# The first norm of a hybrid decoder layer: unit-stride normalisation, norm weights spread over the partitions by the tensor engine, and another written order up to the keys and values

## The chip, the core and the metric

The kernel runs on one core of a Trainium2 chip. The core has a tensor engine (PE) for matrix products, a vector engine (DVE), a scalar engine (ACT), GpSimd (POOL) and a sync engine (SP) that here issues nearly all the DMAs. The metric is the device time of one execution in microseconds (us), and less is better.

## The reference, cut to what matters

One decoder layer over 512 tokens of width 1024: a norm, a projection by `w_in`, two attention branches, an output projection with a residual, then a mixture of experts and a last norm. The change touches the first norm and the first columns of the projection.

```python
def rms_norm(x, g):
    xf = x.astype(jnp.float32)
    y = xf * lax.rsqrt(jnp.mean(xf * xf, axis=-1, keepdims=True) + EPS)
    return (y * g.astype(jnp.float32)).astype(x.dtype)
...
    proj = h @ w_in
    q_f, k_f, v_f, f_logit, q_s, k_s, v_s, gl_f, gl_s = jnp.split(proj, SPLIT_POINTS, axis=-1)
...
        h = rms_norm(x, attn_norm[l])
        x = x + hybrid_mixer(h, positions, w_in[l], b_forget[l], b_gate[l], attn_sinks[l],
                             w_proj_fox[l], w_proj_swa[l], w_out[l])
        h = rms_norm(x, ffn_norm[l])
        x = x + hier_moe(h, w_group[l], b_group[l], w_expert[l], b_expert[l], w1[l], w3[l], w2[l])
    return rms_norm(x, final_norm)
```

## The kernel before

The 512 tokens are four tiles of 128 (t = 0 to 3); the width of 1024 is eight chunks of 128, in two halves of four chunks (k = 0, 1). A product in full precision is made of three matrix products of rounded parts: every operand is split into a high part (a copy with rounding, on ACT) and a low part (the operand less its high part, a subtraction). `mm3` (lines 298 to 301) issues the three: high by high, high by low weights, low activations by high weights.

From line 386 on the order is written by hand: each of PE, DVE, ACT, POOL and SP takes its instructions in the order in which the Python code issues them (`tc.manual_schedule`). An instruction that waits holds up all that stand behind it on its engine.

**Loads.** SP issues x tile 0, the norm weights `gn` (one row read for each of 128 partitions, 512 KB), the two weight units `kv_0` and `kv_1` (each 4 chunks of 256 columns and 8 more, line 172), x tile 1, small inputs, x tiles 2 and 3, then the first unit of the sliding-window queries (`qs0_0`). Three raw buffers and three pairs of split buffers (pools `raw` and `ws`) go round: `next_unit` (line 193) splits the next unit (`hi` on ACT at line 185, `lo` on DVE, or on GpSimd for `kv_1`, line 186) and issues another load.

**The first norm.** `mean_square(t)` squares a tile on ACT with the sum as a by-product (line 242), then finds the reciprocal root: one small DVE instruction, a power on GpSimd (line 230), four more small DVE instructions (lines 231 to 234). `norm(t)` multiplies x, the root and the weights in two DVE instructions of 512 columns (line 251), reading x and writing `hn` with strides, since chunk c here holds the columns c, c+8, c+16 and so on. `transpose_h(t)` turns the tile by four PE transposes per half (line 257), and each half is split into `hT_hi` on ACT (line 260) and `hT_lo` on DVE (line 261).

**Keys and values.** For each tile, 24 products (8 chunks by 3) against `kv_0` and `kv_1` build one accumulator of 264 columns. After the fourth chunk of tile t (`START_T`) stand the transposes of tile t+1 and then the norm of tile t+2, so that a norm is written more than a tile ahead of its transposes. A tile's result is read out by one ACT copy and two DVE instructions (lines 417 to 419). The unit `qs0_0` is split after tile 1, the positions are cast to floats there (line 422), and six steps of the rotary angles (`angles`, with two small PE transposes at lines 271 and 272) stand between tiles 2 and 3. 30 transposes of the identity (line 396) run at the very start. After tile 3 come two more units, the rest of the angles, the masks, and the products of the queries (`acc_qs`).

Of the kernel before, what the change touches and what calls it, by code (L numbers as in the profile page):

```python
# [11 lines left out]
F32 = mybir.dt.float32  # L12
# [3 lines left out]
AF = mybir.ActivationFunctionType  # L16
OP = mybir.AluOpType
# [14 lines left out]
UNIT = 264  # L32
# [8 lines left out]
LAG = (2, 3)  # L41
WAIT = 2
REST = (2, 3)
START_T = 3
WARM = 30
ANGLES_AT = 6
FORGET_AT = 13
ROUNDS = 5
# [22 lines left out]
def bcast_rows(ap, n):  # L71

    return bass.AP(tensor=ap.tensor, offset=ap.offset, ap=[[0, P], [1, n]])
# [24 lines left out]
def kernel(ctx: ExitStack, tc: tile.TileContext, a: dict, out: bass.AP, dbg=None):  # L98
    nc = tc.nc
    pools = Pools(tc)  # L100
    ctx.callback(pools.close_all)
    v, act, pe, gp = nc.vector, nc.scalar, nc.tensor, nc.gpsimd
    dbg = dbg or {}

    x2 = a["x"][0]
    out2 = out[0]
    w_in = a["w_in"][0]
# [17 lines left out]
    def o_tile(name):  # L125
        return ps.tile([P, 512], F32, tag="o", name=name, bufs=2)
# [4 lines left out]
    ssq, rinv, rtmp = cst[:, 16:20], cst[:, 20:24], cst[:, 24:32]  # L131
    mcst = main.tile([P, 64], F32, name="mcst")
    sinks, bgate, pos, bfor, neg_sinks = (mcst[:, x:y] for x, y in ((0, 8), (8, 24), (24, 28), (32, 40), (40, 48)))
# [1 line left out]
    stage_i = xin.tile([P, P], I32, name="stage_i")  # L135
    bg_rows, inv_rows = stage[:16, 0:128], stage[:, 128:160]
    x_sb = [xin.tile([P, D], F32, tag=f"x{t}", name=f"x_sb{t}") for t in range(NT)]
    gn = xin.tile([P, D], F32, name="gn")
    w_in_pc = w_in.rearrange("(p c) n -> p c n", c=NC)


    units = {}
    for name in ORDER:
        kind, i = name.rstrip("0123456789"), int(name[-1]) if name[-1].isdigit() else 0
# [47 lines left out]

    def next_unit(wait=0):

        if len(halves_of) < len(unit_names):
            key = unit_names[len(halves_of)]
            halves_of[key] = split(raws[key], key, wait)
            load_unit()

    nc.sync.dma_start(x_sb[0], x2[0:P, :])  # L200
    nc.sync.dma_start(gn, bcast_rows(a["attn_norm"][0], D))
    load_unit()
    nc.sync.dma_start(x_sb[1], x2[P:2 * P, :])
    load_unit()
    nc.sync.dma_start(stage_i[:NT, :], a["positions"][0].rearrange("(t p) -> t p", p=P))
    nc.sync.dma_start(inv_rows, bcast_rows(a["inv_freq"], 32))
    nc.sync.dma_start(bg_rows, a["b_gate"][0].rearrange("g (b p) -> (g b) p", p=P))
    nc.sync.dma_start(bfor, bcast_rows(a["b_forget"], 8))
    nc.sync.dma_start(sinks, bcast_rows(a["attn_sinks"], NH))
    for t in range(2, NT):  # L210
        nc.sync.dma_start(x_sb[t], x2[t * P:(t + 1) * P, :])
    load_unit()
    nc.sync.dma_start(g_ffn, a["ffn_norm"][0].rearrange("(p c) -> p c", c=NC))

    ident = const.tile([P, P], F32, name="ident")
    make_identity(nc, ident)
    mhalf = const.tile([P, NT], F32, name="mhalf")
# [7 lines left out]
    def rsqrt_mean(dst, ssq, tmp):  # L225

        n = ssq.shape[-1]
        ms, e = tmp[:, 0:n], tmp[:, n:2 * n]
        v.tensor_scalar(ms, ssq, 1.0 / D, EPS, op0=OP.mult, op1=OP.add)
        gp.tensor_tensor(dst, ms, mhalf[:, 0:n], op=OP.pow)  # L230
        v.tensor_tensor(e, dst, dst, op=OP.mult)
        v.tensor_tensor(e, e, ms, op=OP.mult)
        v.tensor_scalar(e, e, -0.5, 1.5, op0=OP.mult, op1=OP.add)
        v.tensor_tensor(dst, dst, e, op=OP.mult)

    hn = [xin.tile([P, NC, P], F32, tag=f"hn{t}", name=f"hn{t}") for t in range(NT)]
    hT_hi = main.tile([P, NC, T], F32R, name="hT_hi")
    hT_lo = main.tile([P, NC, T], F32R, name="hT_lo")
    xt = xin.tile([P, 2 * NT], F32, name="xt")

    def mean_square(t):
        act.activation(hn[t].rearrange("q c p -> q (c p)"), x_sb[t], AF.Square, accum_out=ssq[:, t:t + 1])
        rsqrt_mean(rinv[:, t:t + 1], ssq[:, t:t + 1], xt[:, 2 * t:2 * t + 2])

    def norm(t):

        r = rinv[:, t:t + 1]
        x_pc, g_pc = (z.rearrange("q (p c) -> q p c", c=NC) for z in (x_sb[t], gn))
        h_pc = hn[t].rearrange("q c p -> q p c")
        for c in (slice(0, 4), slice(4, 8)):  # L250
            v.scalar_tensor_tensor(h_pc[:, :, c], x_pc[:, :, c], r, g_pc[:, :, c], op0=OP.mult, op1=OP.mult)

    def transpose_h(t):
        for k in range(2):
            pst = pt_tile(f"hT_ps{t}_{k}")
            for c in range(4):
                pe.transpose(pst[:, c * P:(c + 1) * P], hn[t][:, 4 * k + c], ident)
            d = (slice(None), slice(4 * k, 4 * k + 4), slice(t * P, (t + 1) * P))
            p3 = pst.rearrange("p (c n) -> p c n", c=4)
            act.activation(hT_hi[d], p3, AF.Copy)  # L260
            v.tensor_tensor(hT_lo[d], p3, hT_hi[d].bitcast(F32), op=OP.subtract)
# [36 lines left out]
    def mm3(o, l_hi, l_lo, r_hi, r_lo, first, last):  # L298
        pe.matmul(o, l_hi, r_hi, start=first, stop=False, skip_group_check=True)  # L299
        pe.matmul(o, l_hi, r_lo, start=False, stop=False, skip_group_check=True)  # L300
        pe.matmul(o, l_lo, r_hi, start=False, stop=last, skip_group_check=True)  # L301
# [86 lines left out]
    vs = main.tile([P, NT, P], F32, name="vs")  # L388
# [3 lines left out]


    warm = o_tile("warm")
    for _ in range(WARM):
        pe.transpose(warm[:, 0:P], ident, ident)
    mean_square(0)
    norm(0)
    next_unit()
    transpose_h(0)  # L400
    mean_square(1)
    next_unit()
    norm(1)
    mean_square(2)
    for t in range(NT):
        s = slice(t * P, (t + 1) * P)
        o = acc_tile(f"acc_kv_{t}")[:, :UNIT]
        for cc in range(NC):
            hi, lo = halves_of[f"kv_{cc // 4}"]
            mm3(o, hT_hi[:, cc, s], hT_lo[:, cc, s], hi[:, cc % 4], lo[:, cc % 4], cc == 0, cc == NC - 1)  # L410
            if cc == START_T and t + 1 < NT:
                transpose_h(t + 1)
                if t + 2 < NT:
                    norm(t + 2)
                if t == 0:
                    mean_square(3)
        act.activation(ks_r[:, t].rearrange("p h d -> p (h d)"), o[:, 0:128], AF.Copy)
        v.tensor_copy(vs[:, t], o[:, 128:256])
        v.tensor_tensor(fz[:, t], o[:, 256:264], bfor, op=OP.add)
        if t == 1:  # L420
            next_unit()
            v.tensor_copy(posf, stage_i[:NT, :])
        if t == 2:
            turns = angles()
            for _ in range(ANGLES_AT):
                next(turns)
    for _ in range(2):
        next_unit()
    for _ in turns:
# [533 lines left out]
    for n in range(4):  # L963
# [5 lines left out]
        for m, src_hi, src_lo in (("pf", lambda k: ofT[k][0], lambda k: ofT[k][1]),  # L969
                                  ("ps", lambda k: osT_hi[:, k], lambda k: osT_lo[:, k])):  # L970
            hi, lo = halves_of[f"{m}{n}"]
            for j in range(2):
                b = 2 * n + j
                o = acc_tile(f"{m}_ps{b}")
                for k in range(4):
                    s = slice(j * P, (j + 1) * P)
# [224 lines left out]
    g_ps = [acc_tile(f"g_ps0_{k}") for k in range(2)]  # L1201
# [254 lines left out]
    for b in range(N_BATCH):  # L1456
# [20 lines left out]
        if b == 0:  # L1477
# [6 lines left out]
            g_ps = [acc_tile(f"g_ps1_{k}") for k in range(2)]  # L1484
# [67 lines left out]
```

## Time and profile before

| | us |
|---|---|
| median of 3 runs (1319.5 to 1320.19) | 1320.0 |
| the profiled execution | 1320.74 |
| its span in the trace | 1318.6 |
| outside the span (launch and end) | 2.1 |

Busy over the whole span: PE 1124.6 us (85%), DVE 461.0 (35%), ACT 244.4 (19%), POOL 74.4 (6%). The 16 DMA engines are busy over 90% in nearly every slice of the last two thirds and much less in the first third. The granted PE clock is given as a share of 2.4 GHz: 0.50 is 1.2 GHz. Of the chain of work that ended last, 62% is PE and 30% DMA, the latter all in the loading of expert weights. A share over the whole span says little of the first 33 us, with which the change deals; they have to be read as a stage of their own, together with the question of whether anything later can take up what they lose or win.

### The profile page before, as it was taken

To read this page: it belongs to the slowest core of one execution; us is meant where nothing else is said; L and a number is where in the kernel's file an instruction comes from. 1 tells how busy PE (TensorE), PEld (TensorE's weight loads), DVE (VectorE), ACT (ScalarE), POOL (GpSimd) and SP (SyncE) were. 2 spreads that over 40 slices of the span, in tenths; PEclk is the share of its full clock that TensorE was granted. 3 is DMA by queue.
4 is the path that set the end of the run, shared out by engine and by line. 5 is a ranking of instruction groups with operands and counts; after the bars stand their busy time and mean duration, and the time that the engine had idled before them with its cause. 6 is when DMAs were issued, how large, how long until landed. Compare 5 with 4: busy or idle time off the path is not lost.

```text
span 1318.6 us, 16874 instructions
## 1 busy us (share of the span) xinstructions
PE 1124.6 (85%) x6930; PEld 612.3 (46%) x6930; DVE 461.0 (35%) x1145; ACT 244.4 (19%) x554; POOL 74.4 (6%) x102
## 2 busy tenths in 40 slices
PE   7999999999999797968779786968788786968865
PEld 7997777887994253413233231413232331413212
DVE  6777666226362263212213122212213122211203
ACT  4655444423541000000000000000000000000003
POOL 2600000002000000000000000000000000000002
PEclk8999999999999889989889898889889899989979
DMA  5312332247789999999999999999999999999995
GB/s 178 97 49 74 82 90 65 80 106 255 300 282 399 426 428 421 425 428 427 427 427 426 426 429 427 427 425 424 428 426 428 427 428 425 426 427 424 428 421 189
DMA packets 69704, 439.44 MB, mean 333 GB/s; under 512 B 9893, under 2 KB 39609, under 8 KB 44154
## 3 DMA queue, kind: packets, MB, share of 16 engines
q1 hardware_dynamic: 69626, 438.34, 82.0%
q8 instruction: 56, 0.92, 0.3%
q14 instruction: 22, 0.18, 0.0%
HBM read 434.00 MB, written 2.10 MB: 331 GB/s over the span
## 4 chain that ended last, share of the span: by engine, by line
PE 62%; DMA 30%; DVE 3%; issue 1%; SPq 1%; POOL 1%; ACT 0%; DVEq 0%; POOLq 0%; ACTq 0%
DMA load<-in_w_dram 30%; PE h L1466 11%; PE y_ps L1503 9%; PE g_ps L1154 9%; PE c_ps L1260 8%; PE acc_g L299 2%; PE acc_g L300 2%; PE acc_g L301 2%; SPq L935 1%; PE of_ps L730 1%; PE acc_wo L301 1%; PE acc_wo L299 1%; PE acc_wo L300 1%; PE fpT_ps L712 1%; PE acc_qf L299 1%
## 5 line engine op out<-in xcount | busy, mean ns | idle before, releaser
L1466 PE MATMUL h<-load,u_hi 128*32 128x512 f32 x1920 | 292.2, 673 | 91.9 <-DMA load<-in_w_dram 91.9
L1503 PE MATMUL y_ps<-load,u_hi 128*32 128x512 f32 x920 | 165.7, 670 | 55.7 <-DMA load<-in_w_dram 52.4
L1466 PEld LDWEIGHTS h<-load,u_hi 128*32 128x32 f32 x1920 | 69.3, 122 | 291.1 <-issue 157.4
L1154 PEld LDWEIGHTS g_ps<-u_hi,xc 128*128 128x128 f32 x1024 | 118.7, 194 | 24.3 <-issue 12.5
L1154 PE MATMUL g_ps<-u_hi,xc 128*128 128x128 f32 x1024 | 124.9, 280 | 0.9 <-DVE u_hi L1108 0.8
L1266 DVE TENSOR_TENSOR u_lo<-c_ps,u_lo 128x512 f32<-128x512 f32 x84 | 58.1, 691 | 188.3 <-PE c_ps L1260 188.3
L1503 PEld LDWEIGHTS y_ps<-load,u_hi 128*32 128x32 f32 x920 | 40.2, 117 | 169.0 <-issue 87.4
L1157 DVE TENSOR_TENSOR u_hi<-g_ps,cst 128x512 f32<-128x512 f32 x32 | 21.8, 683 | 273.7 <-PE h L1466 258.6
L1260 PE MATMUL c_ps<-xb,xb 128*128 128x512 f32 x240 | 116.7, 617 | 1.0 <-DVE u_lo L1263 0.8
L1247 ACT ACTIVATE xb<-h 128x512 f32<-128x512 f32 x16 | 9.6, 597 | 355.7 <-PE h L1466 355.7
L1260 PEld LDWEIGHTS c_ps<-xb,xb 128*128 128x128 f32 x240 | 37.8, 188 | 79.4 <-DVE u_lo L1266 36.8
L1235 POOL TENSOR_TENSOR xb<-xb,u_hi 128x512 f32<-128x512 f32 x16 | 20.3, 1270 | 824.3 <-DVE xb L1234 745.6
L1257 ACT ACTIVATE xb<-y_ps 128x512 f32<-128x512 f32 x30 | 17.9, 597 | 216.1 <-PE y_ps L1503 216.1
L1254 ACT ACTIVATE u_hi<-t_ps 128x512 f32<-128x512 f32 x16 | 9.6, 597 | 254.2 <-PE t_ps L1253 254.2
L299 PE MATMUL acc_g<-hT_hi,hi_g 128*128 128x512 f32 x128 | 54.2, 423 | 0.0
L1104 DVE TENSOR_SCALAR u_hi<-codes,locs,cst 128x128 f32<-128x128 f32 x60 | 21.7, 362 | 87.5 <-PE g_ps L1154 87.5
L300 PE MATMUL acc_g<-hT_lo,hi_g 128*128 128x512 f32 x128 | 50.5, 395 | 0.0
L301 PE MATMUL acc_g<-hT_hi,lo_g 128*128 128x512 f32 x128 | 50.4, 394 | 0.0
L1248 DVE TENSOR_TENSOR u_hi<-h,xb 128x512 f32<-128x512 f32 x16 | 16.5, 1032 | 95.2 <-PE h L1466 94.3
L188 DVE TENSOR_TENSOR lo_g<-raw_g,hi_g 128x1024 fp32r<-128x1024 f32 x16 | 19.6, 1226 | 36.1 <-ACT hi_g L185 36.1
L299 PE MATMUL acc_wo<-hi_wo,mT 128*128 128x256 f32 x96 | 28.7, 299 | 0.0
L301 PE MATMUL acc_wo<-hi_wo,mT 128*128 128x256 f32 x96 | 27.1, 283 | 0.1
(372 smaller groups left out, 1630.2 us busy)
## 6 DMA issues: line engine op xcount, KB each, us to landing
load<-in_w_dram SPq DMA_DIRECT2D x176, 2048.0 KB
first<-in_w_dram SPq DMA_DIRECT2D x16, 1024.0 KB
load<-in_w_dram SPq DMA_DIRECT2D x9, 1024.0 KB
raw_g<-in_w_in_dram SPq DMA_DIRECT2D x16, 512.0 KB
raw_wo<-in_w_out_dram SPq DMA_DIRECT2D x8, 512.0 KB
x_sb<-in_x_dram SPq DMA_DIRECT2D x4, 512.0 KB
raw_qs<-in_w_in_dram SPq DMA_DIRECT2D x4, 512.0 KB
raw_vf<-in_w_in_dram SPq DMA_DIRECT2D x4, 512.0 KB
```

The source lines that it names most:

```text
L188: defer(wait, lambda: eng.tensor_tensor(lo, r, hi.bitcast(F32), op=OP.subtract))
L299: pe.matmul(o, l_hi, r_hi, start=first, stop=False, skip_group_check=True)
L300: pe.matmul(o, l_hi, r_lo, start=False, stop=False, skip_group_check=True)
L301: pe.matmul(o, l_lo, r_hi, start=False, stop=last, skip_group_check=True)
L1104: v.tensor_scalar(sel1[:, t], labels, loc[:, 0, t:t + 1], r, op0=OP.is_equal, op1=OP.mult)
L1154: pe.matmul(g_ps[k][:, c * P:(c + 1) * P], xc[t][:, 4 * k + c], sel1[:, t], start=(t, c) == (0, 0), stop=t == NT - 1, skip_group_check=True)
L1157: v.tensor_tensor(hsel[:, 4 * k:4 * k + 4], g_ps[k].rearrange("p (c n) -> p c n", c=4), g_ffn[:, 4 * k:4 * k + 4, None].to_broadcast([P, 4 ...
L1235: gp.tensor_tensor(wsel, wsel, wtmp, op=OP.add)
L1260: pe.matmul(c_ps, w_t[:, t], ys[k], start=True, stop=True)
L1266: v.tensor_tensor(d, c_ps, d, op=OP.add)
L1466: pe.matmul(o[s], hsel[:, c, s], wt[b, m, e][c], start=c == 0, stop=c == NC - 1, skip_group_check=True)
L1503: pe.matmul(y_ps[k][s], gT[:, c, s], wt[b, "w2", e][c][:, 512 * k:512 * k + 512], start=c == 0, stop=c == 3, skip_group_check=True)
```

## The change

- **Chunks without strides.** A chunk now holds 128 neighbouring columns (`(c p)` in place of `(p c)` in the view of `w_in`), so `norm(t, k)` reads and writes 512 neighbouring columns. Its weights are read from PSUM (`g_ps`).
- **Weights of the norm.** The 512 KB load `gn` goes. ACT's queue loads one row of 4 KB, and two products of a row of ones with that row put it on all partitions. They stand between 14 and 6 warming transposes (30 before).
- **Loads.** SP issues x tile 0, `kv_0`, x tile 1, `kv_1`, x tiles 2 and 3, `b_forget`, `qs0_0`, and only then the other small inputs.
- **Written order.** Squares, roots, norm halves, transposes, high and low parts are functions of their own and are written out one by one. The roots of tiles 2 and 3 are found together. A half of a tile has its 12 products in one go (`kv_products`), grouped by term. For tiles 2 and 3 there is a loop: norm, transposes, high part and low part of half 0, the same of half 1, then 24 products. In tile 3, ahead of its products, stand the split of `qs0_0`, the cast of the positions and the first step of the angles.
- **Read-out.** The values are copied out by ACT in place of DVE.

Line 186, which names the engine of the subtraction for `kv_1`, is not among the changed lines.

```diff
-WARM = 30
+WARM = (14, 6)
...
-    gn = xin.tile([P, D], F32, name="gn")
-    w_in_pc = w_in.rearrange("(p c) n -> p c n", c=NC)
+    sq_out = xin.tile([P, D], F32, name="sq_out")
+    g_row = xin.tile([1, D], F32, name="g_row")
+    ones = xin.tile([1, P], F32, name="ones")
+    w_in_pc = w_in.rearrange("(c p) n -> p c n", c=NC)
...
+    nc.scalar.dma_start(g_row, a["attn_norm"])
+    for t in range(2):
+        nc.sync.dma_start(x_sb[t], x2[t * P:(t + 1) * P, :])
+        load_unit()
+    for t in range(2, NT):
+        nc.sync.dma_start(x_sb[t], x2[t * P:(t + 1) * P, :])
+    nc.sync.dma_start(bfor, bcast_rows(a["b_forget"], 8))
     load_unit()
...
+    g_ps = [s_tile(f"g_norm{k}") for k in range(2)]
+    def spread_weights(k):
+        pe.matmul(g_ps[k], ones, g_row[:, 512 * k:512 * k + 512], start=True, stop=True)
+    def squares(t):
+        act.activation(sq_out, x_sb[t], AF.Square, accum_out=ssq[:, t:t + 1])
+    def factors(t, n):
+        return rsqrt_mean(rinv[:, t:t + n], ssq[:, t:t + n], xt[:, 2 * t:2 * t + 2 * n])
+    def norm(t, k):
+        d = slice(512 * k, 512 * k + 512)
+        v.scalar_tensor_tensor(hn[t][:, d], x_sb[t][:, d], rinv[:, t:t + 1], g_ps[k], op0=OP.mult, op1=OP.mult)
...
+    def kv_products(t, k):
+        if k == 0:
+            kv_ps[t] = acc_tile(f"acc_kv_{t}")[:, :UNIT]
+        o, s = kv_ps[t], slice(t * P, (t + 1) * P)
+        hi, lo = halves_of[f"kv_{k}"]
+        terms = ((hT_hi, hi), (hT_hi, lo), (hT_lo, hi)) if (t, k) == (0, 0) else ((hT_hi, hi), (hT_lo, hi), (hT_hi, lo))
+        for i, (l, r) in enumerate(terms):
+            for c in range(4):
+                pe.matmul(o, l[:, 4 * k + c, s], r[:, c], start=(k, i, c) == (0, 0, 0), stop=(k, i, c) == (1, 2, 3),
+                          skip_group_check=True)
+    def kv_evac(t):
+        o = kv_ps[t]
         act.activation(ks_r[:, t].rearrange("p h d -> p (h d)"), o[:, 0:128], AF.Copy)
-        v.tensor_copy(vs[:, t], o[:, 128:256])
+        act.activation(vs[:, t], o[:, 128:256], AF.Copy)
         v.tensor_tensor(fz[:, t], o[:, 256:264], bfor, op=OP.add)
+    def high_unit():
+        before = len(deferred)
+        next_unit(1)
+        return deferred.pop(before)[1]
+    warm_up(WARM[0])
+    for k in range(2):
+        spread_weights(k)
+    warm_up(WARM[1])
+    squares(0)
+    f = factors(0, 1)
+    next(f)
+    next(f)
+    norm(0, 0)
+    transpose_h(0, 0)
+    norm(0, 1)
+    low = high_unit()
+    h_high(0, 0)
+    low()
+    transpose_h(0, 1)
+    h_low(0, 0)
+    squares(1)
+    f = factors(1, 1)
+    next(f)
+    kv_products(0, 0)
+    h_high(0, 1)
+    h_low(0, 1)
+    low = high_unit()
+    next(f)
+    norm(1, 0)
+    low()
+    kv_products(0, 1)
+    transpose_h(1, 0)
+    squares(2)
+    norm(1, 1)
+    h_high(1, 0)
+    squares(3)
+    h_low(1, 0)
+    f = factors(2, 2)
+    kv_evac(0)
+    transpose_h(1, 1)
+    h_high(1, 1)
+    kv_products(1, 0)
+    next(f)
+    h_low(1, 1)
+    next(f)
+    kv_products(1, 1)
+    for t in (2, 3):
+        for k in range(2):
+            norm(t, k)
+            transpose_h(t, k)
+            h_high(t, k)
+            if t == 3 and k == 0:
+                kv_evac(1)
+            h_low(t, k)
+        if t == 3:
+            low = high_unit()
+            low()
             v.tensor_copy(posf, stage_i[:NT, :])
             turns = angles()
+            next(turns)
+        for k in range(2):
+            kv_products(t, k)
+    kv_evac(2)
+    for _ in range(ANGLES_AT - 1):
+        next(turns)
+    kv_evac(3)
     for _ in range(2):
         next_unit()
```

## Rows read from the trace of the kernel before

**Rows 1.** Busy us by stage: stretch, length, PE, PEld, DVE, ACT, POOL, clock, DMA, GB/s
```profile
33.20:58.00 24.80, 24.80 (x213) 24.73 (x212) 18.83 (x46) 17.72 (x43) 14.35 (x31) 1.00 0.30 87
...
130.00:300.00 170.00, 169.75 (x908) 130.37 (x906) 84.64 (x166) 70.82 (x144) 5.18 (x10) 1.00 0.33 90
300.00:410.00 110.00, 107.50 (x807) 91.08 (x806) 60.63 (x218) 43.99 (x114) 10.33 (x11) 1.00 0.79 285
410.00:1280.00 870.00, 700.08 (x4154) 271.67 (x4158) 208.50 (x490) 44.93 (x78) 19.96 (x16) 0.92 1.01 426
```

**Rows 2.** All waits of PE from 33 to 300 us: total, times, longest
```profile
PE qsT_ps L500 <- DVE qs_st L495: 0.3, 1, 0.3
PE fpT_ps L712 <- ACT fp L700: 0.3, 1, 0.3
```

**Rows 3.** PE in order of time: start, length; tile 2's transposes, the first query product
```profile
23.18 1.04 PE L257 MATMUL hT_ps<-ident,hn 128*128 128x128 f32 x8
...
33.20 0.28 PE L299 MATMUL acc_qs<-hi_qs,hT_hi 128*128 128x256 f32 x1
```

**Rows 4.** Chain of work that ended last, 10 to 34 us: start, share of chain, what
```profile
12.97 2.34 DVE xt L232
...
15.72 1.12 DVE hn L251
...
16.98 2.03 PE hT_ps L257 x8
19.00 0.22 PE acc_kv L299
...
23.82 0.61 ACT hT_hi L260
...
25.06 0.68 DVE hT_lo L261
...
28.54 0.12 PE acc_kv L299
```

**Rows 5.** ACT, DVE and POOL in order of time, the first 15 us
```profile
4.52 1.06 ACT L242 ACTIVATE hn<-x_sb 128x1024 f32<-128x1024 f32 x1 [2.44 <-DMA x_sb<-in_x_dram]
7.18 0.16 DVE L234 TENSOR_TENSOR cst<-cst,xt 128x1 f32<-128x1 f32 x1
8.47 1.08 ACT L185 ACTIVATE hi_kv<-raw_kv 128x1056 fp32r<-128x1056 f32 x1 [2.79 <-DMA raw_kv<-in_w_in_dram]
11.73 1.07 ACT L185 ACTIVATE hi_kv<-raw_kv 128x1056 fp32r<-128x1056 f32 x1
12.87 2.42 POOL L190 TENSOR_TENSOR lo_kv<-raw_kv,hi_kv 128x1056 fp32r<-128x1056 f32 x1
```

**Rows 6.** DVE and PE in order of time: query weights, positions, second angle transpose
```profile
27.87 1.22 DVE L190 TENSOR_TENSOR lo_qs<-raw_qs,hi_qs 128x1024 fp32r<-128x1024 f32 x1
29.00 0.21 DVE L422 CAST stage<-stage_i 4x128 f32<-4x128 int32 x1
...
30.01 0.20 PE L272 MATMUL pst<-ident,stage 4*128 4x4 f32 x1
```

**Rows 7.** Lines 659 and 1522, by form: count, shortest/median/longest ns, starts
```profile
L659 DVE SCALAR_TENSOR_TENSOR fq<-acc_qf,fq x8: 683/689/693, 108.5 to 174.1; 64x512 fp32r<-64x512 f32 x8
...
L1522 PE MATMUL fnorm_ps<-u_raw,one_row x4: 1056/1056/1218, 688.8 to 691.5; 1*128 1x512 f32 x4
```

**Rows 8.** Stretches with PE's granted clock: stretch, length, PE busy, clock, DMA, GB/s
```profile
17.00:22.00 5.00, 5.00 (x23) 0.50 0.78 251
22.00:23.00 1.00, 1.00 (x10) 0.98 0.00 0
621.00:626.00 5.00, 1.04 (x2) 1.00 1.03 439
626.00:628.00 2.00, 0.00 (x0) 0.55 1.00 426
...
644.00:648.00 4.00, 1.01 (x6) 1.00 1.00 426
```

More of the change, by code (lines that the diff above doesn't have):

```diff
@@ L43 @@
 REST = (2, 3)
-START_T = 3
-WARM = 30
+WARM = (14, 6)
 ANGLES_AT = 6
@@ L198, in next_unit @@
             load_unit()
[L200 to L203, printed above, removed]
+    nc.scalar.dma_start(g_row, a["attn_norm"])
[5 more added lines that the diff above has]
+    nc.sync.dma_start(bfor, bcast_rows(a["b_forget"], 8))
     load_unit()
@@ L207 @@
     nc.sync.dma_start(bg_rows, a["b_gate"][0].rearrange("g (b p) -> (g b) p", p=P))
-    nc.sync.dma_start(bfor, bcast_rows(a["b_forget"], 8))
     nc.sync.dma_start(sinks, bcast_rows(a["attn_sinks"], NH))
-    for t in range(2, NT):
-        nc.sync.dma_start(x_sb[t], x2[t * P:(t + 1) * P, :])
-    load_unit()
     nc.sync.dma_start(g_ffn, a["ffn_norm"][0].rearrange("(p c) -> p c", c=NC))
+    v.memset(ones, 1.0)
     ident = const.tile([P, P], F32, name="ident")
@@ L230, in rsqrt_mean @@
         gp.tensor_tensor(dst, ms, mhalf[:, 0:n], op=OP.pow)
+        yield
         v.tensor_tensor(e, dst, dst, op=OP.mult)
@@ L234, in rsqrt_mean @@
         v.tensor_tensor(dst, dst, e, op=OP.mult)
-    hn = [xin.tile([P, NC, P], F32, tag=f"hn{t}", name=f"hn{t}") for t in range(NT)]
+        yield
+    hn = [xin.tile([P, D], F32, tag=f"hn{t}", name=f"hn{t}") for t in range(NT)]
     hT_hi = main.tile([P, NC, T], F32R, name="hT_hi")
@@ L239, with transpose_h, h_part, h_high @@
     xt = xin.tile([P, 2 * NT], F32, name="xt")
[L241 to L261, printed above, removed]
+    g_ps = [s_tile(f"g_norm{k}") for k in range(2)]
[8 more added lines that the diff above has]
+        v.scalar_tensor_tensor(hn[t][:, d], x_sb[t][:, d], rinv[:, t:t + 1], g_ps[k], op0=OP.mult, op1=OP.mult)
+    hT_ps = {}
+    def transpose_h(t, k):
+        pst = hT_ps[t, k] = pt_tile(f"hT_ps{t}_{k}").rearrange("p (c n) -> p c n", c=4)
+        for c in range(4):
+            pe.transpose(pst[:, c], hn[t][:, (4 * k + c) * P:(4 * k + c + 1) * P], ident)
+    def h_part(t, k):
+        return slice(None), slice(4 * k, 4 * k + 4), slice(t * P, (t + 1) * P)
+    def h_high(t, k):
+        act.activation(hT_hi[h_part(t, k)], hT_ps[t, k], AF.Copy)
+    def h_low(t, k):
+        d = h_part(t, k)
+        v.tensor_tensor(hT_lo[d], hT_ps[t, k], hT_hi[d].bitcast(F32), op=OP.subtract)
     ang = main.tile([P, 2, NT, 32], F32, name="ang")
@@ L394, with warm_up @@
     warm = o_tile("warm")
[L395 to L416, printed above, removed]
+    def warm_up(n):
+        for _ in range(n):
+            pe.transpose(warm[:, 0:P], ident, ident)
@@ new lines @@
+    kv_ps = {}
+    def kv_products(t, k):
[5 more added lines that the diff above has]
+        for i, (l, r) in enumerate(terms):
+            for c in range(4):
+                pe.matmul(o, l[:, 4 * k + c, s], r[:, c], start=(k, i, c) == (0, 0, 0), stop=(k, i, c) == (1, 2, 3),
+                          skip_group_check=True)
@@ L417 @@
+    def kv_evac(t):
+        o = kv_ps[t]
         act.activation(ks_r[:, t].rearrange("p h d -> p (h d)"), o[:, 0:128], AF.Copy)
-        v.tensor_copy(vs[:, t], o[:, 128:256])
+        act.activation(vs[:, t], o[:, 128:256], AF.Copy)
         v.tensor_tensor(fz[:, t], o[:, 256:264], bfor, op=OP.add)
-        if t == 1:
-            next_unit()
+    def high_unit():
[5 more added lines that the diff above has]
+        spread_weights(k)
@@ L422 @@
+    squares(3)
[20 more added lines that the diff above has]
+            low()
             v.tensor_copy(posf, stage_i[:NT, :])
-        if t == 2:
@@ L424 @@
             turns = angles()
-            for _ in range(ANGLES_AT):
-                next(turns)
+            next(turns)
[5 more added lines that the diff above has]
+    kv_evac(3)
     for _ in range(2):
```

## The prediction, made before the changed kernel was run

> **What bounds the kernel now.** I read the table by stages first. From 33.2 to 300 us the tensor engine is busy without a break [rows 1], and the list of its waits in that stretch holds two of 0.3 us each [rows 2]. From 300 to 410 us it is still 98% busy; from 410 us the loads of expert weights run at 1.01 of the DMA engines' share [rows 1]. Those loads go into buffers that earlier work frees, so their start hangs on the tensor engine too. The reader is to see that there is no slack behind the keys and values into which a shift could vanish: whatever moves the first query product, which starts at 33.20 us [rows 3], moves the end by as much. So the question is one number: when does that product start in the changed kernel? Call it E. I then read the chain of waits up to E and the engines' timelines.
>
> Two things make E late today. DVE's small instruction of line 232, 0.16 us elsewhere, takes 2.34 us [rows 4] just while GpSimd runs its 2.42 us subtraction [rows 5]; tile 1's norm and transposes wait for it until 16.98 us. And the granted clock is then 0.50 (1.2 GHz) until 22 us [rows 8], so a product takes 0.22 us in place of 0.12 [rows 4].
>
> **What the change takes away early.** A norm half costs 1.12 us with strides [rows 4]. The new one has unit stride and one operand in PSUM; the nearest row is the same operation with a PSUM operand and 512 columns, 0.69 us [rows 7]. So 0.43 us less for each half on the chain. With `gn` gone, 512 KB less lies ahead of the weights. `kv_1` was there by 11.73 us [rows 5] and has to be there at 10.9 now; I take it that it is, and price the other case at up to +1.0.
>
> The spreading of the weights isn't in this stage's trace. Two such products last 1.06 us each [rows 7], up to double at half clock. x tile 0 lands at 4.5 us [rows 5]; if the 4 KB row, issued at the same time, is there by then, the weights are spread well before the first norm needs them at 7.34 [rows 5]: cost nothing, hidden behind squares and root. If it came only with `kv_0` at 8.47 [rows 5], they would be ready some 2 to 3 us late: E +1.6 to +2.5. I take nothing, since the row is small and its queue empty. No run here shows a load from ACT's queue; the Trainium skill (DMA: Bandwidth & Descriptors, section on queues, rings and completion order) has the DMA engines take turns between the rings of SP and ACT, and by it the cost is nothing.
>
> **The chain up to tile 2, step by step.** Squares 4.52 to 5.68, root as today, first norm half at 7.35 to 8.05, transposes (0.14 wait, 0.60) to 8.8, high part 0.60 to 9.4. ACT's order then has the squares of tile 1 (1.06) ahead of the second half's high part: 10.35 to 10.95. The high part of `kv_1` (1.07) follows, to 11.95.
>
> Line 186 is not in the diff, so the subtraction for `kv_1` is still GpSimd's, 2.42 us from 12.0 to 14.4. DVE meanwhile does the low part of tile 0's second half (from 11.0, 0.61) and starts tile 1's four small instructions at 11.6; the fourth would start at 12.2, and is held to 14.4 as line 232 is today [rows 4]. So tile 1's norm starts at 14.6 (15.72 today [rows 4]), its transposes at 15.4 in place of 16.98, at half clock.
>
> By the Trainium skill (SBUF — State Buffer, section on who interferes with whom) a DVE instruction is held by GpSimd's SBUF reads if two of its inputs lie in SBUF. The norm with its weights in PSUM is then free of it, and only the small instruction stalls. If that one got through before 12.0, E would be 0.1 (half clock) to 0.7 us (full) earlier.
>
> Next, tile 0's last four products wait for the subtraction and end at 15.5. Tile 1: transposes 15.4 to 17.4; 12 products at 0.22 from 17.2; tile 3's squares stand ahead of the second half's high part on ACT (18.5 to 19.1), so its low part ends at 19.8 and the root of tiles 2 and 3 at 20.5. Tile 1's other 12 products end at 21.6 if the clock rises about 5 us after tile 1's transposes begin, as it does today (16.98 to 22 us [rows 4, 8]). Tile 2's transposes start at 21.6, against 23.18 today [rows 3]: **1.5 us ahead.**
>
> **What the change adds late.** Today the norm of a tile is written a tile ahead. The new loop for tiles 2 and 3 writes norm, transposes, high, low of half 0 and only then the norm of half 1. DVE can't start that norm before the low part, which waits for ACT's high part, which waits for the transposes. One round is: transposes 0.60 + 0.04, high part 0.60 + 0.05 [rows 4], low part 0.61 (0.68 with its tail [rows 4]), norm 0.69 [rows 7], 0.14 to the transposes: 2.73 us. Within it PE has 0.45 us of work, and nothing else may pass: its next instruction is the other half's transposes. So PE stands still for 2.3 us in tile 2 and again in tile 3.
>
> Then comes the longest wait. Ahead of tile 3's products stand the two angle transposes; line 272's needs the cast of the positions, which DVE has behind the low part of `qs0_0`. Today that cast lies off the path, a unit earlier [rows 6]. Now, after tile 3's second transposes: 0.64 to the high part's start, 0.50 until ACT takes the next, 1.05 for the high part of `qs0_0`, 0.05, then 1.22 (1.14 to the next) for its low part and 0.21 for the cast [rows 6], 0.1 to PE: 3.7 us from the transposes' start, of which PE works 0.45.
>
> The sum, from 21.63: second transposes of tile 2 at +2.73 = 24.36; 0.44 for them, 24 products x 0.1225 = 2.94 [rows 4]: 27.74; tile 3's first transposes there, the second at 30.47; +3.7 = 34.16 line 272; 0.2; products from 34.36. At full clock 24 x 0.1225 gives E = 37.3, **4.1 us later** than 33.20.
>
> **The clock in the late part.** From 28.2 to 34.3 us PE would work 0.6 us in 6. The nearest rows: with 1.04 us of work in 621 to 626 the clock fell after 626 to 0.55; with 1.01 in 644 to 648 it stayed [rows 8]. The gap here is the longer kind, so I take a fall. Today the rise came behind 5 us of steady work [rows 8]; if it comes as late here or somewhat sooner, 15 to 20 of the products take 0.22: +1.3 to +1.9, I take 1.5. E = 38.8, **5.6 us later**.
>
> The smaller parts: the early loss of half clock is in the sum. The copies moved from DVE to ACT cost ACT 0.19 each; the last delays the split of the next query unit by that, which is needed 5.8 us later (48 products). The small inputs come later on SP's queue, but are needed only from 17 us. `qs1_1`'s load waits for the low part of `qs0_0` (33.9 in place of 29.1) and is needed some 7 us after E: hidden.
>
> So 1320.74 + 5.6 = 1326.3 for an execution like the profiled one, which lies 0.74 above the median; against the median, 1320.0 + 5.6 = **1325.6 us**.
>
> **The rivals.**
> (a) The late stalls come as worked out, but the clock stays up, as in the 644 row [rows 8]: E 37.3, 1324.1. Speaks for it that PE works once in the gap; against it the gap's 6 us.
> (b) Half clock from 12 us right through, because the stalls from 21 us on don't let it rise: all 72 products of tiles 1 to 3 at 0.22, E 42.5, 1329.3. The steady 6 us from 15.4 speak against it.
> (c) The wait for the positions doesn't fall on PE (3.0 us, and the clock's 1.5 with it): E 34.3, 1321.1. It decides if line 272's transpose has its data before the second half's transposes are through.
> (d) Faster: the engines don't keep the written order where I think they do, so that the norms of tiles 2 and 3 pass the low parts ahead of them and the cast passes the split. Then the three stalls go (2.3 + 2.3 + 3.0) and the late half clock (1.5): E 29.7, 1316.5. The point that decides is whether tile 2's second norm starts before its first low part. Against it: today the cast, whose data come from an early load, stands at 29.00, right behind the 27.87 subtraction [rows 6].
> (e) The change doesn't do what it says: its words name no GpSimd subtraction, the diff leaves it. Were it on DVE (1.26 us) and GpSimd free, E would be 0.1 to 0.7 us earlier, as above; nothing of the late part changes.
>
> **How the numbers follow.** Forecast 0.45; (a) 0.24; (b) 0.08; (c) 0.12; (d) 0.11; (e) lies inside the forecast's spread. A measurement of this kernel can tell about 0.2%, 2.6 us, from no change. Slower by more: forecast, (a), (b): 0.77. Same: (c), 0.12. Faster: 0.11. The range reaches from (c), 1321, to (b), 1329.5; it holds the late row of the norm's weights too (1325.6 + 2.5) and leaves out (d) and the outer edges of (b) and (c).
>
> **What would show it.** In the profile after: DVE's norm of tile 2's second half starting behind its first low part; PE idle near 2.3 us twice and near 3 us before line 272's transposes; a small DVE instruction stretched to about 2 us beside GpSimd's subtraction; the first query product at 37 to 39 us; from there the same stretches as today. Wrong if the query product starts before 35 us, or if it starts late and the end doesn't follow.

## The result

| | before | after |
|---|---|---|
| median, us | 1320.0 (1319.5 to 1320.6) | 1328.0 (1327.0 to 1328.8, 5 runs) |
| profiled execution, us | 1320.74 | 1327.79 |
| its span, us | 1318.6 | 1325.3 |
| first query product (E), us | 33.20 | 41.11 |

The ratio of after to before is 1.0061, with a 95% interval of 1.0046 to 1.0076: the change makes the kernel 8.0 us slower. The forecast was 1325.6 us, with a range of 1321.0 to 1329.5.

PE in order of time shows where the time went (start and length in us, engine, line, output from inputs, count, and in brackets the idle time before the row and what ended it).

```profile
4.60 3.78 PE L247 MATMUL g_norm<-g_row,ones 1*128 1x512 f32 x4
8.31 1.54 PE L412 MATMUL warm<-ident 128*128 128x128 f32 x6
9.64 1.92 PE L265 MATMUL hT_ps<-ident,hn 128*128 128x128 f32 x8
...
17.29 1.28 PE L265 MATMUL hT_ps<-ident,hn 128*128 128x128 f32 x8
...
22.73 0.63 PE L265 MATMUL hT_ps<-ident,hn 128*128 128x128 f32 x4 [0.29 <-DVE hn L258]
25.51 0.63 PE L265 MATMUL hT_ps<-ident,hn 128*128 128x128 f32 x4 [2.16 <-DVE hn L258]
...
28.90 0.60 PE L265 MATMUL hT_ps<-ident,hn 128*128 128x128 f32 x4
32.07 0.63 PE L265 MATMUL hT_ps<-ident,hn 128*128 128x128 f32 x4 [2.57 <-DVE hn L258]
...
35.72 0.27 PE L286 MATMUL pst<-ident,stage 4*128 4x4 f32 x1 [2.86 <-DVE stage L493]
35.91 1.25 PE L425 MATMUL acc_kv<-hi_kv,hT_hi 128*128 128x264 f32 x4
...
41.11 0.28 PE L313 MATMUL acc_qs<-hi_qs,hT_hi 128*128 128x256 f32 x1
```

Tile 2's transposes (22.73) are 0.45 us ahead of those of before [rows 3]. From there on PE stands still three times, 2.16, 2.57 and 2.86 us, and tile 3's 24 products, from 35.91 to 41.11, take 0.22 us each. E is 7.91 us later than before.

Behind E the kernel runs as before, shifted. The same stretches as in [rows 1], taken 8 us later (stretch, length, busy us with counts of PE, PEld, DVE, ACT, POOL, granted clock, DMA share, GB/s; 0.50 is 1.2 GHz), with the two in which the time is lost ahead of them:

```profile
22.00:33.00 11.00, 5.84 (x45) 4.98 (x43) 4.69 (x8) 2.40 (x6) 0.00 (x0) 1.00 0.01 1
34.00:40.00 6.00, 4.28 (x19) 4.27 (x20) 3.23 (x11) 0.61 (x3) 2.23 (x6) 0.50 0.32 87
...
41.11:65.91 24.80, 24.80 (x213) 24.73 (x212) 18.47 (x45) 17.88 (x44) 14.32 (x30) 1.00 0.30 87
138.00:308.00 170.00, 169.74 (x908) 130.61 (x906) 84.63 (x166) 70.80 (x144) 5.19 (x10) 1.00 0.33 92
308.00:418.00 110.00, 107.54 (x808) 91.13 (x806) 60.68 (x218) 43.99 (x114) 10.34 (x11) 1.00 0.79 283
```

In 22 to 33 us PE works 5.84 of 11 us. From 41 to 418 us each stretch shown holds PE's load of its like in [rows 1], and the list of PE's waits up to 300 us again holds the two of 0.3 us of [rows 2]: there nothing is made up. Behind that, in the loading of the expert weights, executions differ. E is 7.91 us later, the end 7.05 in the two profiled executions and 8.0 in the medians; over the twelve kernels profiled here the time less E lies between 1285.9 and 1289.4 us. So a difference of a microsecond or two between two kernels need not come from the stretch ahead of E.

DVE's rows show what each wait is made of (columns as for PE).

```profile
14.07 2.29 DVE L236 TENSOR_TENSOR cst<-cst,xt 128x1 f32<-128x1 f32 x1
16.40 1.40 DVE L258 SCALAR_TENSOR_TENSOR hn<-x_sb,cst,g_norm 128x512 f32<-128x512 f32 x2
...
24.02 0.69 DVE L275 TENSOR_TENSOR hT_lo<-hT_ps,hT_hi 128x512 fp32r<-128x512 f32 x1 [1.44 <-ACT hT_hi L271]
24.63 0.74 DVE L258 SCALAR_TENSOR_TENSOR hn<-x_sb,cst,g_norm 128x512 f32<-128x512 f32 x1
...
30.51 0.17 DVE L432 TENSOR_TENSOR f_sb<-acc_kv,mcst 128x8 f32<-128x8 f32 x1 [2.35 <-ACT vs L431]
30.59 0.68 DVE L275 TENSOR_TENSOR hT_lo<-hT_ps,hT_hi 128x512 fp32r<-128x512 f32 x1
31.19 0.74 DVE L258 SCALAR_TENSOR_TENSOR hn<-x_sb,cst,g_norm 128x512 f32<-128x512 f32 x1
...
34.31 1.23 DVE L189 TENSOR_TENSOR lo_qs<-raw_qs,hi_qs 128x1024 fp32r<-128x1024 f32 x1 [0.25 <-ACT hi_qs L186]
35.45 0.21 DVE L493 CAST stage<-stage_i 4x128 f32<-4x128 int32 x1
```

The norm of tile 2's second half (24.63) starts behind the low part of its first half (24.02), in tile 3 likewise (31.19 behind 30.59), and the cast of the positions (35.45) behind the low part of `qs0_0`. The small instruction of line 236 is held for 2.29 us; GpSimd's subtraction runs from 13.91 for 2.43 us.

### The profile page after: what moved, and what is told of

Read it like the earlier page. It is cut to its first block, busy times and chain, and to the rows that moved or that the text cites. A ratio compares the mean times of both kernels' runs of the same rounds, so it can differ in the third digit from the quotient of the medians.

```text
span 1325.3 us, 16857 instructions
## 1 busy us (share of the span) xinstructions
PE 1131.7 (85%) x6924; PEld 614.7 (46%) x6924; DVE 458.2 (35%) x1137; ACT 244.6 (18%) x558; POOL 74.3 (6%) x101
## 4 chain that ended last, share of the span: by engine, by line
PE 62%; DMA 28%; DVE 4%; issue 2%; ACT 1%; SPq 1%; POOL 1%; DVEq 0%; POOLq 0%; ACTq 0%
DMA load<-in_w_dram 28%; PE h L1541 11%; PE y_ps L1578 9%; PE g_ps L1229 9%; PE c_ps L1335 8%; PE acc_g L313 2%; PE acc_g L314 2%; PE acc_g L315 2%; PE of_ps L805 1%; SPq L1010 1%; PE acc_wo L315 1%; PE acc_wo L313 1%; PE acc_wo L314 1%; PE fpT_ps L787 1%; PE acc_kv L425 1%
```

## The experiments

Ten kernels ran: eight edits of the kernel after and two of the kernel before. E is the start of the first query product in the profiled execution; times are medians, ratios are to runs of the kernel before on the same chip.

| kernel | E, us | time, us (runs) | ratio, 95% |
|---|---|---|---|
| before | 33.20 | 1320.0 | |
| after | 41.11 | 1328.0 (5) | 1.0046 to 1.0076 |
| e1_norms_ahead | 36.01 | 1323.2 (10) | 1.0010 to 1.0029 |
| e2_angles_later | 36.79 | 1324.7 (7) | 1.0025 to 1.0048 |
| e3_filled_gaps | 37.26 | 1324.7 (5) | 1.0024 to 1.0052 |
| e4_subtraction_on_dve | 41.51 | 1329.8 (4) | 1.0054 to 1.0087 |
| e5_no_second_warmup | 41.21 | 1328.5 (5) | 1.0049 to 1.0076 |
| e7_all_mended | 30.34 | 1319.15 (11) | 0.9983 to 1.0001 |
| e8_gaps_filled_dve | 38.43 | 1325.8 (5) | 1.0027 to 1.0053 |
| e9_gaps_filled_gpsimd | 37.08 | 1325.9 (4) | 1.0029 to 1.0060 |
| e6_unit_stride_only | 32.30 | 1318.8 (11) | 0.9982 to 1.0000 |
| e10_kv1_subtraction_on_dve | 30.07 | 1316.9 (8) | 0.9964 to 0.9985 |

**The norms, written ahead.** The theory: the serial order of norm, transposes and low part in the new loop makes two waits on PE and most of the loss. The edit takes only that order away; the angles keep their place.

```diff
-    for t in (2, 3):
-        for k in range(2):
-            norm(t, k)
-            transpose_h(t, k)
...
+    norm(2, 0)
+    norm(2, 1)
+    transpose_h(2, 0)
+    h_high(2, 0)
+    transpose_h(2, 1)
+    h_high(2, 1)
+    h_low(2, 0)
+    norm(3, 0)
+    h_low(2, 1)
+    norm(3, 1)
+    kv_products(2, 0)
+    transpose_h(3, 0)
...
+    kv_evac(1)
+    kv_products(2, 1)
+    transpose_h(3, 1)
...
```

> The changed kernel with the loop over tiles 2 and 3 written so that each norm half stands ahead of the previous tile's low parts; the angles stay where the change put them. Theory (the written order makes PE wait 2.16 and 2.57 us for line 258's norm): both waits go, the first query product comes 4.7 us earlier than 41.11, about 1323.3 us; 2.2 us more, 1321.1, if with a shorter idle stretch the clock doesn't fall. Rival (PE waits there for something that the order doesn't set, and the loss is elsewhere): under 1 us, 1327 to 1328.

It took 1323.2 us, as the theory had it (the profiled execution, with 1324.8, was the longest of the ten), and E was 36.01, 5.1 us earlier. PE in order of time, from tile 2 on:

```profile
22.74 1.29 PE L265 MATMUL hT_ps<-ident,hn 128*128 128x128 f32 x8 [0.29 <-DVE hn L258]
...
25.86 0.60 PE L265 MATMUL hT_ps<-ident,hn 128*128 128x128 f32 x4
...
27.75 0.60 PE L265 MATMUL hT_ps<-ident,hn 128*128 128x128 f32 x4
...
31.37 0.26 PE L286 MATMUL pst<-ident,stage 4*128 4x4 f32 x1 [2.85 <-DVE stage L503]
```

The waits of 2.16 and 2.57 us are gone, and tile 3's second transposes stand at 27.75 in place of 32.07. The wait for the positions stays to the hundredth (2.85 against 2.86). So the two norm rounds cost 4.3 us on PE's path; the rest of the 5.1 us is clock: in 31 to 35 us it is 0.57 here, and 1.00 from 35 us on, so that only about half of tile 3's products are slow.

**The angles, moved behind the products.** The theory: the cast of the positions makes the third wait.

```diff
-        if t == 3:
-            low = high_unit()
-            low()
-            v.tensor_copy(posf, stage_i[:NT, :])
-            turns = angles()
-            next(turns)
         for k in range(2):
             kv_products(t, k)
+    low = high_unit()
+    low()
+    v.tensor_copy(posf, stage_i[:NT, :])
+    turns = angles()
+    next(turns)
```

> The changed kernel with the split of qs0_0, the cast of the positions and the first angle step written behind tile 3's products. Theory (PE stands 2.86 us before the second angle transpose for the cast): that wait goes, first query product 3.1 us earlier, 1324.9 us; 1322.7 if the clock then stays at full. Rival (the split of qs0_0 is needed anyway and the wait only moves to the first query product): under 1 us, 1327 to 1328.

It took 1324.7 us, near the theory's 1324.9. Line 286 stands at 36.16 behind the products and waits for nothing; tile 3's products start 0.38 us behind the second transposes, at 32.90, at full clock.

```profile
32.52 0.63 PE L265 MATMUL hT_ps<-ident,hn 128*128 128x128 f32 x4 [2.57 <-DVE hn L258]
32.90 0.74 PE L425 MATMUL acc_kv<-hi_kv,hT_hi 128*128 128x264 f32 x4
...
36.16 0.22 PE L286 MATMUL pst<-ident,stage 4*128 4x4 f32 x1
```

But now the clock fell in tile 2 (stretches as above):

```profile
22.00:25.00 3.00, 0.84 (x8) 0.63 (x6) 1.35 (x2) 0.60 (x1) 0.00 (x0) 0.96 0.00 0
25.00:28.00 3.00, 3.00 (x15) 3.00 (x15) 1.34 (x2) 0.60 (x1) 0.00 (x0) 0.50 0.02 5
28.00:36.00 8.00, 5.43 (x44) 5.09 (x42) 3.35 (x6) 2.81 (x7) 0.00 (x0) 0.99 0.00 0
```

The wait of 2.16 us ahead of it is the same as in the kernel after, where the clock stayed at 1.00 until 33 us. The same gap can cost the clock or not.

That the time meets the theory is in part luck. With tile 3 at full clock the theory had 1322.7 us. In this execution the clock rose earlier at the start, which put tile 2's transposes 1.11 us ahead (21.62 against 22.73); the fall in tile 2 took 1.54 back (24.41 to 29.34 is 4.93 us, 3.39 in the kernel after); and from tile 3's second transposes to E it is 4.27 us in place of 9.04.

**The clock alone.** Here all waits stay, and PE turns the identity meanwhile: 18 transposes in tile 3's norm round and 22 ahead of the angles.

```diff
             h_high(t, k)
             if t == 3 and k == 0:
+                warm_up(18)
                 kv_evac(1)
...
             v.tensor_copy(posf, stage_i[:NT, :])
+            warm_up(22)
             turns = angles()
```

> The changed kernel with 18 and 22 transposes of the identity in PE's two idle stretches of tile 3; no wait is taken away. Theory (the idle 6 us let the clock fall to 0.50, and tile 3's 24 products pay 2.2 us for it): the products run at 0.12 us each, the first query product 2.0 to 2.3 us earlier, 1325.8 us. Rival (they are slow because of their order by term, or the clock falls all the same): 0, or up to 0.5 us slower, 1328 to 1328.5.

It took 1324.7 us, more of a gain than expected. PE in order of time, and the clock:

```profile
27.70 2.13 PE L412 MATMUL warm<-ident 128*128 128x128 f32 x18
30.43 0.63 PE L265 MATMUL hT_ps<-ident,hn 128*128 128x128 f32 x4 [0.60 <-DVE hn L258]
30.89 2.56 PE L412 MATMUL warm<-ident 128*128 128x128 f32 x22
...
34.08 0.22 PE L286 MATMUL pst<-ident,stage 4*128 4x4 f32 x1 [0.46 <-DVE stage L494]
34.23 0.75 PE L425 MATMUL acc_kv<-hi_kv,hT_hi 128*128 128x264 f32 x4
```
```profile
12.00:38.00 26.00, 21.03 (x161) 18.82 (x160) 14.98 (x33) 8.22 (x21) 5.37 (x8) 1.00 0.24 72
```

The useful work comes at the same distances (30.43 is 3.17 us behind tile 3's first transposes at 27.26, as in the kernel after), and the clock is 1.00 throughout. Tile 3's products take 34.23 to 37.26, 3.03 us in place of 5.20: the late clock costs 2.17 us. The other 1.66 us of E's gain was there before the first fill: tile 2's transposes stood at 21.07, since the clock rose earlier at the start of this execution (last section).

**The subtraction on DVE.** The rival that the change doesn't do what it says: its words name no GpSimd subtraction, but line 187 still sends `kv_1`'s to GpSimd. The edit does what the words say.

```diff
-        eng = gp if name == "kv_1" else v
+        eng = v
```

> The changed kernel with the subtraction for kv_1 on DVE, as its words say and its diff doesn't. Theory (GpSimd's subtraction holds one small DVE instruction for 2.29 us, but tile 0's last products wait for the same subtraction wherever it runs, so it costs little): the small instruction takes 0.16 us again, tile 1's transposes start 0.3 to 0.6 us earlier, end 0.1 to 0.7 us earlier, 1327.3 to 1327.9 us. Rival (the held instruction is on the path with its whole 2.1 us): about 1325.9 us.

It took 1329.8 us, and both sides missed. From tile 2 on the waits on DVE's norm are the same 5.0 us in sum and the one for the positions 2.8, but the clock fell twice:

```profile
25.00:28.00 3.00, 3.00 (x16) 3.00 (x16) 1.32 (x2) 0.00 (x0) 0.00 (x0) 0.50 0.00 0
...
32.00:41.00 9.00, 6.20 (x28) 5.74 (x28) 3.87 (x11) 1.87 (x4) 2.22 (x6) 0.50 0.19 58
```

Tile 2's transposes stand at 20.89, 1.84 us ahead of the kernel after, most of it since here too the clock rose earlier (x's first transposes are 1.41 us ahead); the fall in tile 2 and the longer one in tile 3 take that back, and E is 41.51, 0.40 us later. So the falls account for 0.4 of the 1.8 us that this kernel takes longer. At the start of `out_ps` it is 0.5 us (379.0 against 378.5); the rest arises behind that, and what it is stays open.

To tell the subtraction from the clock, the next two kernels fill all three gaps (15 transposes in tile 2 beside the 18 and 22), one with the subtraction on DVE, one on GpSimd.

```diff
             transpose_h(t, k)
             h_high(t, k)
+            if k == 0:
+                warm_up((15, 18)[t - 2])
...
+            warm_up(22)
             turns = angles()
```

> The changed kernel with identity transposes in PE's idle stretches of tiles 2 (15) and 3 (18 and 22), and kv_1's subtraction on DVE. Beside e9 it shows what the subtraction's place costs when the clock is held. Theory (e4 lost its 1.8 us to a clock that fell in tile 2 and stayed low in tile 3; the place itself gains a little): 0.1 to 0.7 us faster than e9. Rival (the subtraction on DVE itself loses time, by its 1.26 us in DVE's queue): 1 to 2 us slower than e9.

> As e8, with kv_1's subtraction on GpSimd as in the changed kernel. Theory: the clock stays at full from tile 1 on, the first query product at 37 to 38.5 us, 1324 to 1325.5 us, as e3. Rival (transposes of the identity don't hold the clock in tile 2): as e3 or up to 1.5 us slower.

They took 1325.8 and 1325.9 us. The second met its E and missed its time by 0.4. In both, the clock is 1.00 from 15 to 38 us. Their E can't be compared, since the clock rose later at the start of the first (the spread of the weights takes 3.78 us there, 2.33 in the second). From the start of tile 0's transposes to that of tile 2's it is 12.60 us on DVE (9.65 to 22.25) and 12.70 on GpSimd (8.20 to 20.90), first on DVE, then on GpSimd:

```profile
9.65 1.91 PE L265 MATMUL hT_ps<-ident,hn 128*128 128x128 f32 x8
...
22.25 0.63 PE L265 MATMUL hT_ps<-ident,hn 128*128 128x128 f32 x4 [0.29 <-DVE hn L258]
```
```profile
8.20 1.77 PE L265 MATMUL hT_ps<-ident,hn 128*128 128x128 f32 x8 [0.46 <-DVE hn L258]
...
20.90 0.63 PE L265 MATMUL hT_ps<-ident,hn 128*128 128x128 f32 x4 [0.31 <-DVE hn L258]
```

So in this written order the place of the subtraction is worth about 0.1 us, by the traces and by the medians, and with the gaps filled e4's kernel is 4.0 us faster.

**Without the six transposes.** At the start PE does the spread of the weights (3.78 us) and six more transposes, and x's first transposes stand behind them.

```diff
-WARM = (14, 6)
+WARM = (14, 0)
```

> The kernel after without the six identity transposes that it writes behind the spread of the norm's weights. Theory: they stand in TensorE's order ahead of the first transposes of x and delay them by their own 1.54 us where the clock has not yet risen, and by nothing where the transposes wait for the norm in any case; the late products move up by as much. Between 1326.7 and 1327.7 us, first query product at 39.8 to 41.1 us. Rival: the six transposes hold TensorE at work, and without them the clock rises later or falls earlier: 1328 us or more, with a granted clock under 1.00 in more of the first 45 us.

It took 1328.5 us, no gain: the rival's side. The trace shows both at work. x's first transposes start at 8.31 in place of 9.64, and tile 2's came 1.27 us earlier (21.46 against 22.73), as the theory had it; then the clock took it back. PE and the clock's stretches:

```profile
8.31 2.03 PE L265 MATMUL hT_ps<-ident,hn 128*128 128x128 f32 x8
...
21.46 0.63 PE L265 MATMUL hT_ps<-ident,hn 128*128 128x128 f32 x4 [0.30 <-DVE hn L258]
24.25 1.08 PE L265 MATMUL hT_ps<-ident,hn 128*128 128x128 f32 x4 [2.16 <-DVE hn L258]
24.99 1.23 PE L425 MATMUL acc_kv<-hi_kv,hT_hi 128*128 128x264 f32 x4
```
```profile
24.00:27.00 3.00, 2.75 (x13) 2.78 (x14) 1.10 (x3) 0.60 (x1) 0.00 (x0) 0.50 0.02 5
...
34.00:40.00 6.00, 4.18 (x19) 4.17 (x20) 3.33 (x11) 0.72 (x3) 2.23 (x6) 0.50 0.30 87
```

Tile 2's second transposes to tile 3's first take 4.75 us (24.25 to 29.00) in place of 3.39.

**All of it mended.** The norms ahead, the angles behind the products, the subtraction on DVE and no second warming: what the rest of the change (unit stride, spread weights, order of loads) is worth beside these.

> The changed kernel with the norm halves written ahead, the angles behind tile 3's products, kv_1's subtraction on DVE and no transposes of the identity behind the spreading. Theory (the change's parts are worth having and its late written order alone loses): tile 2's transposes at 20.5 to 21.5 us, then 48 products and 12 transposes' worth with no waits, first query product at 29 to 30.5 us, 1316 to 1317.5 us; up to 1319 if the clock falls somewhere. Rival (the early part is no faster than before either): 1320 us or more.

E came as expected, at 30.34, 10.8 us earlier than after; its last 0.50 us is a wait for DVE:

```profile
30.34 0.35 PE L313 MATMUL acc_qs<-hi_qs,hT_hi 128*128 128x256 f32 x1 [0.50 <-DVE f_sb L432]
```

The time, 1319.15 us, is 1.65 us above the 1316 to 1317.5 expected for such an E, though the clock is at 1.00 from 15 to 30 us; its interval reaches over 1, so it isn't clearly faster than before. Of E's lead of 2.9 us over before, 2.5 are left at 131.2 us (the start of `acc_g`, 133.7 before) and at 368.0 (`out_ps`, 370.5 before); the rest goes between there and the end, in the loading of the expert weights and behind it. What it is stays open.

**The first norm's strides alone.** Two edits of the kernel before follow. The first does only the unit stride, with `gn` in SBUF.

```diff
-    w_in_pc = w_in.rearrange("(p c) n -> p c n", c=NC)
+    w_in_pc = w_in.rearrange("(c p) n -> p c n", c=NC)
...
-            v.scalar_tensor_tensor(h_pc[:, :, c], x_pc[:, :, c], r, g_pc[:, :, c], op0=OP.mult, op1=OP.mult)
+            v.scalar_tensor_tensor(h[:, d], x_sb[t][:, d], r, gn[:, d], op0=OP.mult, op1=OP.mult)
```

> The kernel before with one part of the change alone: chunks of neighbouring columns, so that the norm's two instructions read and write without strides; gn, the loads and the written order stay. Theory (the unit stride is worth 0.37 us for each half on the chain, which holds one half of tile 0, one of tile 1 and two of tile 3): 1.12 us falls to 0.75 us, the first query product comes 0.4 to 1.4 us earlier, 1318.6 to 1319.6 us. Rival (a change in the chunks' layout slows the loads of w_in or another reader): 1320 us or more.

It took 1318.8 us with E at 32.30: 0.9 us earlier, 1.1 us faster, as expected, though the interval just reaches 1. The two norm halves of a tile take 1.41 us here with the weights in SBUF and 1.40 in the kernel after with the weights in PSUM (2.05 before): it is the stride that shortens them, not the place of the weights.

The second adds the subtraction on DVE, written behind the norm of tile 1.

```diff
-        eng = gp if name == "kv_1" else v
+        eng = v
...
     mean_square(1)
-    next_unit()
     norm(1)
+    next_unit()
     mean_square(2)
```

> The kernel before with norms without strides, and with the subtraction for tile 1's key and value low parts moved from GpSimd to VectorE, written behind the norm of tile 1. Theory: without the GpSimd subtraction VectorE's work is no longer held for its length (2.43 us in the kernel after), against 1.26 us more on VectorE itself: the first query product comes 1 to 2 us earlier than the 32.3 us of e6_unit_stride_only, and the time is 1317 to 1318.5 us. Rival: VectorE's own instruction takes the place of the hold, and nothing moves: 1318.8 us as e6_unit_stride_only, or more, with the first query product at 32.3 us or later.

It took 1316.9 us, 3.1 us less than before and 1.9 us less than the unit stride alone. DVE in order of time, first of e6_unit_stride_only, then of e10_kv1_subtraction_on_dve:

```profile
12.84 2.36 DVE L231 TENSOR_TENSOR xt<-cst 128x1 f32<-128x1 f32 x1 [0.68 <-POOL cst L230]
...
15.82 1.41 DVE L250 SCALAR_TENSOR_TENSOR hn<-x_sb,cst,gn 128x512 f32<-128x512 f32 x2
```
```profile
12.97 0.16 DVE L231 TENSOR_TENSOR xt<-cst 128x1 f32<-128x1 f32 x1 [0.68 <-POOL cst L230]
...
13.74 1.41 DVE L250 SCALAR_TENSOR_TENSOR hn<-x_sb,cst,gn 128x512 f32<-128x512 f32 x2
15.08 1.25 DVE L190 TENSOR_TENSOR lo_kv<-raw_kv,hi_kv 128x1056 fp32r<-128x1056 f32 x1
```

The same small instruction takes 0.16 us where GpSimd doesn't subtract and 2.36 where it does; tile 1's norm starts 2.08 us earlier, E is 2.23 us earlier. Between the two the clock differs as well: tile 1's products run slowly until 17.3 us in the second and until 21.5 in the first, which puts tile 2's transposes 2.98 us ahead (19.84 against 22.82), and 0.75 of that is lost again by E. This is the fastest of all kernels here, and it has none of the new written order, spread weights or order of loads.

## Why the prediction was right, and where its sizes were off

The mechanism was the predicted one, and its signs are in the profile: three waits on PE near 2.3, 2.3 and 3 us (2.16, 2.57, 2.86), a DVE instruction stretched to about 2 us (2.29), the late fall of the clock, and an end that moves with E (7.91 us at E, 8.0 in the medians, 7.05 in the profiled pair). One sign failed: E was to come at 37 to 39 us, 38.8 in the sum, and came at 41.11. So the way was right and the sum too small. The 2.3 us between them, term by term:

| term | forecast | measured | difference |
|---|---|---|---|
| tile 2's first transposes start | 21.63 | 22.73 | +1.10 |
| to its second transposes (a norm half takes 0.74, not 0.69) | 2.73 | 2.78 | +0.05 |
| 24 products, to tile 3's first | 3.38 | 3.39 | +0.01 |
| to tile 3's second | 2.73 | 3.17 | +0.44 |
| to line 272, now 286 | 3.69 | 3.65 | -0.04 |
| to the products | 0.20 | 0.19 | -0.01 |
| tile 3's 24 products | 4.44 | 5.20 | +0.76 |

**The spread of the weights was priced wrongly.** "Two such products last 1.06 us each" misread its own row: that row of [rows 7] counts four instructions for two products, at a granted clock of 0.50 (688 to 690 us), so two products are four instructions of 1.06 us. Its "up to double at half clock" comes to nearly the same 4.2 us, but by luck. The step that failed is the next one: the prediction asked only when the norm has its weights, and they were in time (the 4 KB row too, since PE starts the spread at 4.60, right behind the 14 transposes, with no wait for the load). What it left out is PE's own order: the four instructions took 3.78 us and, with six transposes behind them, held x's first transposes until 9.64 us, 8.2 in the prediction's sum. "Cost nothing, hidden behind squares and root" holds where the clock rises early: in e3_filled_gaps the four take 2.23 us, x's transposes stand at 8.21, and tile 2's at 21.07.

**The early clock was better than assumed, the hold on DVE came later.** The subtraction on GpSimd started at 13.91 in place of 12.0, as all before it was late, so the held instruction (2.29 us, about 2.2 in the prediction) ended at 16.36, and tile 1's transposes stood at 17.29 and not at 15.4. But tile 1's products ran at 0.12 us, not at half clock; that gave back about 0.8 of the 1.9 us.

**An instruction was overlooked.** Tile 3's round is 0.44 us longer than forecast, and 0.39 longer than tile 2's. The trace puts that down to the read-out of tile 1, which stands in it: DVE's 30.51 row waits for ACT's copy of the values and holds the low part. No run takes it away by itself. In the kernel before, ACT makes one copy; the change added the second, which the prediction priced on ACT alone.

**The clock's price was too low.** The fall was right, "15 to 20 of the products" was not: it stayed at 0.50 from 34 to 40 us, and nearly all 24 ran slow. The fills price it at 2.17 us against the forecast's 1.5. That the clock fell once and not twice was luck: the prediction has no fall in tile 2, and in e2, e4 and e5 one came behind the same gap there.

The rivals. (a), a clock that stays up, is e3_filled_gaps: 1324.7 us, where (a) said 1324.1, but not what the kernel did. (b), half clock throughout, came only for tile 3's products: tiles 1 and 2 ran at 0.12 us a product. That the time is nearer to (b)'s 1329.3 than to the forecast is the sum of the other terms, not (b)'s way. (c), a wait for the positions off PE, is e2_angles_later: line 286 waits for nothing there, while in the kernel after it waits 2.86 us. (d), an order in which the norms and the cast pass, had E at 29.7; written by hand in e7_all_mended, with two more edits, it gives 30.34, but 1319.15 us in place of 1316.5. So "moves the end by as much" didn't hold there. (e), the subtraction still on GpSimd, was true and, within this order, worth about 0.1 us (e8, e9), at the lower end of its 0.1 to 0.7.

From tile 2's transposes to E it is 18.38 us after and 9.37 in e7_all_mended (20.97 to 30.34). Of the 9.0 us between, the two norm rounds are 4.3 (e1); the wait for the positions (2.86) and the slow products behind it (2.17, e3), less the 0.5 that e7 itself waits ahead of its query product, make 4.5 of the other 4.7. Before, the same way takes 10.02 us.

## What to carry to other kernels

In an order written by hand, each engine's next instruction has to be ready while another engine works on the last: a loop that reads well (norm, transposes, high, low, one half after the other) ties three engines to one chain, and the product engine waits for each turn of it. Write the norm of the next half ahead of the low part of this one, and put what a small transpose needs a unit earlier or the transpose behind the products. And price a wait on PE with the clock that may go with it: here two gaps of 2.57 and 2.86 us cost 2.17 us more in the products behind them. Taking one early delay away gained nothing here as long as the gaps behind it stayed (e5).

## What the runs showed of the hardware that was not expected

- **The first rise of the clock differs between executions, and the profile's clock column doesn't show it.** The four instructions of the spread take 1.057 us each (median) in the kernel after and 0.588 in e9_gaps_filled_gpsimd, both behind the same 14 transposes. Yet the column prints 1.00 for 4 to 13 us of the kernel after, where its first four products of tile 0 (11.39) are as long, 1.25 us, as the first four at 35.91 under 0.50. Ahead of the first fall in the record, the pace of known products told more than the column here.
- **The same gap of 2.16 us in tile 2 cost the clock in three kernels (e2, e4, e5) and not in two (after, e3).** No run here tells what decides.
- **With transposes of the identity in the gaps the clock stayed up.** With 2.13 and 2.56 us of them in tile 3's two gaps and 0.46 to 0.60 us idle behind, it is 1.00 and tile 3's products take 3.03 us in all three kernels that have them (e3, e8, e9); with both gaps empty it fell in all three (after, e4, e5).
- **Beside a GpSimd subtraction of 2.4 us a 128x1 instruction of two operands on DVE takes nearly as long as it** (2.36 against 0.16 us). In the order of before the swap is worth 1.9 us of the whole (e6, e10); in the written order of the change about 0.1 us (e8, e9).
